# Modulation weights requested ahead of x, first quarter unsplit, norm copies on ACT, another order of the first blocks in a hybrid attention and retention layer

## The chip, the cores and the metric

One core of a Trainium2 chip. The metric is the device time of one execution in microseconds, lower is better; the median of several executions is given. The core has a matrix engine (TensorE, PE), three engines for the rest (VectorE or DVE, ScalarE or ACT, GpSimd or POOL), each of which takes its instructions strictly in order, and queues that move data between memory and the on-chip buffer (the SyncE queue, SP, carries nearly all of them here).

## The reference, cut to what matters

One layer over 2048 latent tokens and 256 context tokens of width 1024: a norm, a modulation computed from the condition vector, one input projection, two groups of heads, an output projection and a last norm. The change touches only the path up to the first projections:

```python
mod = jax.nn.silu(c) @ w_ada[i] + b_ada[i]
mod_c = jax.nn.silu(c_ctx) @ w_ada[i] + b_ada[i]
shift, scale, gate = mod[:, None, :D], mod[:, None, D:2 * D], mod[:, None, 2 * D:]
h_lat = _rmsnorm(x, norm_g[i]) * (1.0 + scale) + shift
h_ctx = _rmsnorm(ctx, norm_g[i]) * (1.0 + scale_c) + shift_c
...
na_q, na_k, na_v, na_g, r_q, r_k, r_v, r_g = _split_proj(h_lat @ w_in)
```

## The kernel before, in words

Matrix products are made of pairs: a number is kept as a rounded high part and the rest as a low part, and a product is high x high + low x high + high x low. So every operand needs a cast (high, on ACT) and a subtraction (low, on DVE or POOL) before PE can use it.

**Blocks and parts.** x comes transposed, in eight parts of 256 tokens (x 0 to x 7; part 8 is the context). Two parts make a block of 512 tokens (`blk[0]` to `blk[3]`, tiles `hhi` and `hlo` for high and low). The 1024 features are eight slices k of 128; half u of a part is k = 4u to 4u + 3.

**Modulation.** The weights w_ada come in four quarters u of four pieces j (`ada_load`, 512 KB each). Quarter u gives shift and scale of k = 2u and 2u + 1. A piece is multiplied by the condition on PE (`ada_mm`, `'m'`, L311) either as plain fp32 or, if its bit in `SPL` is set, as high and low part (`ada_split`, `'s'`, ACT L298, then DVE or POOL L300 by `ALO`). `ada_row` (`'ar'`, L319) copies the result out, `ada_fin` (`'af'`) transposes it on PE (L324) and DVE makes `mods` of it (L329 to L332).

**Norm.** `squares` (`'sq'`) squares a part on ACT (L198) and adds slices on POOL (half 0) and DVE (half 1), L200, L201 and a last addition on DVE, L203. `colsum` (`'cs'`, PE L209), `rstd` (DVE L214, POOL L215), `spread_copy` (DVE L220, both in `'rs'`) and `spread` (`'sp'`, PE L227) make the norm's factor for every token; `spread_mul` (`'mu'`, DVE L241) multiplies it in.

**Scale, shift and split.** For block 0 slice by slice: `prep_first(k)` (`'p'`: ACT L262 writes the high part, DVE L263 scales in place, DVE or POOL L265 the low part by `PFL`). For later blocks half by half: `prep_ab` (`'ab'`, DVE L272 and ACT L274) and `prep_hl` (`'hl'`, ACT L279, then DVE or POOL L283 by `LOV`).

**Key steps.** The first projections are the keys: `window(b)` runs, for block b, four units (two weight groups w0 and w1 of 256 columns, two halves each) of eight slices. A step is one slice of one unit: three matmuls at L363. For block 0 the order of units is the table `STEPS`; for the others unit after unit. Steps are numbered 32 b + n. Low parts of w0 and w1 (tile `wlo`, L347) are made by `w_split` (`'ws'`), on POOL or DVE by `WSL`.

**What sets the order.** `PLAN` is a list written out by hand: (step, action, arguments). After each step's matmuls the actions due at it are issued; those at -1 come ahead of step 0. The engines then run their own instructions in that order and wait only for data, a free buffer or a landed transfer. `LOADS` is the order of the first requests on the SP queue, which land one after the other. Stores and spills of finished blocks (`hS`) share that queue.

Of the kernel before, what the change touches and what calls it, by code (L numbers as in the profile page):

```python
# [9 lines left out]
F32 = mybir.dt.float32  # L10
# [3 lines left out]
ALU = mybir.AluOpType  # L14
# [4 lines left out]
P = 128  # L19
D = 1024  # L20
KC = D // P
# [15 lines left out]
TSQ = {0: 2, 1: 2, 2: 2, 3: 2, 4: 2, 5: 3, 6: 2, 7: 2, 8: 2}  # L37
LOV = {0: 2, 1: 2, 2: 0, 3: 3, 4: 2, 5: 2, 6: 1, 7: 3, 8: 0}
PLAN = [
# [19 lines left out]
]  # L59
SPL = [9, 0, 1, 0]  # L60
ALO = [0, 5, 9, 4]
PFL = [3, 0, 0, 1, 0, 3, 1, 3]
STEPS = [0, 1, 2, 0, 1, 3, 2, 3, 2, 0, 3, 1, 1, 3, 0, 3, 2, 3, 0, 0, 2, 1, 1, 1, 1, 2, 3, 2, 2, 0, 3, 0]
WSL = [3, 2]
LEAD = 32
LOADS = [
# [3 lines left out]
]  # L70
BT = [[(KWIN[i][1] * CWIN[j][1], 0, 0) for j in (0, 1, 3)] for i in (0, 1, 3)]
BN = 0
# [10 lines left out]
def hybrid_kernel(ctx: ExitStack, tc: tile.TileContext, a: dict, out: bass.AP):  # L83
# [22 lines left out]
    ng = cst.tile([P, KC], F32, name="ng")  # L106
    bada = cst.tile([P, 2 * KC], F32, name="bada")
    sil4 = cst.tile([P, KC, 4], F32R, name="sil4")
    mods = cst.tile([P, 4, 3, 2, 2], F32, name="mods")
    one = cst.tile([P, 1], F32, name="one")  # L110
    mhalf = cst.tile([P, 4], F32, name="mhalf")
# [82 lines left out]
    def squares(i):  # L194
        sqs[i] = []
        for u in range(2):
            sq = xsq[i][u] if i < 2 else env["st"].tile([P, KH, 256], F32, name="st")
            nc.scalar.activation(sq, raw[i][u], AF.Square)  # L198
            eng = (nc.gpsimd, nc.vector)[u]
            eng.tensor_tensor(sq[:, 0:2, :], sq[:, 0:2, :], sq[:, 2:4, :], ALU.add)  # L200
            eng.tensor_tensor(sq[:, 0, :], sq[:, 0, :], sq[:, 1, :], ALU.add)  # L201
            sqs[i].append(sq)
        nc.vector.tensor_tensor(sqs[i][0][:, 0, :], sqs[i][0][:, 0, :], sqs[i][1][:, 0, :], ALU.add)  # L203
# [13 lines left out]

    def spread_copy(i):
        rbs[i, 1] = env["st"].tile([P, 2, P], F32, name="t0", bufs=2)
        nc.vector.tensor_copy(rbs[i, 1], rbs[i].unsqueeze(2).to_broadcast([P, 2, P]))  # L220

    def spread(*ii):
        pm = ptile()
# [31 lines left out]
    def prep_first(k):  # L255
        if k == KC - 1:
            spill.extend((i, u, now[0] + 8) for i in range(2) for u in range(2))
        for i in range(2):
            hi, lo = sub_dst(i)
            A, B = ab(i, k)  # L260
            x = raw[i][k // KH][:, k % KH, :]
            nc.scalar.activation(hi[:, k, :], x, AF.Identity, bias=B, scale=A)  # L262
            nc.vector.tensor_scalar(x, x, A, B, ALU.mult, ALU.add)  # L263
            eng = nc.gpsimd if PFL[k] >> i & 1 else nc.vector
            eng.tensor_tensor(lo[:, k, :], x, f(hi[:, k, :]), ALU.subtract)  # L265

    def prep_ab(i, u):
# [25 lines left out]
    def ada_split(u, j):  # L293
        whl[u, j] = []
        for k in range(2):
            w = wad[4 * u + j][:, k, :]
            t = op.tile([P, 2, 512], F32R, name="o")
            nc.scalar.copy(t[:, 0, :], w)  # L298
            eng = nc.gpsimd if ALO[u] >> j & 1 else nc.vector
            eng.tensor_tensor(t[:, 1, :], w, f(t)[:, 0, :], ALU.subtract)  # L300
            whl[u, j].append(t)

    def ada_mm(u, j):
        if u not in aps:
            aps[u] = ptile(psm)
        for k in range(2):
            ops = [(silc, wad[4 * u + j][:, k, :])]
            if SPL[u] >> j & 1:
                ops = [(sil4, whl[u, j][k][:, e, :]) for e in range(2)]
            for i, (s, w) in enumerate(ops):  # L310
                nc.tensor.matmul(aps[u][0:s.shape[2], :], s[:, 2 * j + k, :], w, start=(j == 0 and i == 0 and k == 0),  # L311
                                 stop=(j == 3 and i + 1 == len(ops) and k == 1))
# [3 lines left out]
    def ada_row(u):  # L316
        rows[u] = op.tile([P, 2, 512], F32, name="o")[:, 0, :]
        n = 4 if SPL[u] else 2
        (nc.scalar.copy, nc.vector.tensor_copy)[u % 2](rows[u][0:n, :], aps[u][0:n, :])  # L319

    def ada_fin(u):
        pm, n = ptile(psm), 4 if SPL[u] else 2
# [127 lines left out]
        put_tok(rvS, c0, tp, r)  # L450

    nc.sync.dma_start(silc, a["c2"])
    nc.scalar.activation(silc, silc, AF.Silu)
    nc.scalar.copy(sil4[:, :, 0:2], silc)
    nc.vector.tensor_tensor(sil4[:, :, 2:4], silc, f(sil4[:, :, 0:2]), ALU.subtract)
    nc.vector.memset(one, 1.0)
# [8 lines left out]
    for name, *args in LOADS:  # L465
# [1 line left out]
    acts = dict(sq=squares, cs=lambda *i: colsum(*i), rs=lambda i: (rstd(i), spread_copy(i)), sp=lambda *i: spread(*i),  # L467
                mu=lambda i, u: spread_mul(i, (u,)), ab=prep_ab, hl=prep_hl, blk=alloc_blk, x=load_x, w=lambda: wr.append(w_raw(2560)),
                w2=lambda: load_w(), s=ada_split, m=ada_mm, ar=ada_row, af=ada_fin, p=prep_first,
                ws=lambda g: w01.append(w_split(wr[g], lo=WSL[g])))  # L470
    w01 = []

    def run_acts(n):
        while plan and plan[0][0] <= n:
# [1149 lines left out]
```

## Time and profile before

| | us |
|---|---|
| median of 3 runs | 1368.17 |
| lowest, highest | 1365.89, 1369.72 |
| the profiled execution | 1366.09 |
| its span, first to last instruction | 1364.1 |
| PE busy, to 27.4 us from the start | 17.09 |
| PE busy, 27.4 to 60.4 | 30.62 of 33.0 |
| PE busy, 60.4 to 85 | 22.26 of 24.6 |
| DVE busy, 60.4 to 85 | 21.79 of 24.6 |

A timeline row reads: start in us from the start of the span, time in us, engine, line, operation, output <- inputs, sizes and types, count of merged instructions; in brackets the idle time of the engine just before it and what ended it. Overlapping matmuls each show more than the distance between their starts. A windows row gives a stretch, its length, the busy time and number of instructions, the TensorE clock granted (1 is full), the share of the DMA engines and GB/s. An engine's "busy" time includes time in which it is held up inside an instruction. PE shows an unsplit modulation matmul as two records.

### The profile page before, as it was taken

The numbers are of one execution on the slowest core, as the hardware profiler recorded it, in microseconds if no ns is written. First come the engines' busy times: TensorE is split into PE (matmuls) and PEld (weight loads), VectorE is DVE, ScalarE is ACT, GpSimd is POOL, SyncE is SP. The second block draws the span as 40 slices with busy tenths as digits, with TensorE's granted clock in tenths as the row PEclk, the third lists the DMA queues.
The fourth block names the chain that finished last, engine by engine and source line by source line (L and its number), as shares of the span: only waits on it lengthen the run. The fifth ranks groups of instructions, "written<-read, shape, count | busy, mean of one in ns | idle before, by whom it ended". The sixth has DMA issues, their size and how long they took to land.

```text
span 1364.1 us, 23087 instructions
## 1 busy us (share of the span) xinstructions
PE 1313.1 (96%) x8236; PEld 1148.9 (84%) x8236; DVE 827.9 (61%) x1442; ACT 606.5 (44%) x1259; POOL 583.8 (43%) x571
## 2 busy tenths in 40 slices
PE   6999999999999999999999999999999899999997
PEld 2477899887997788998999889889998789888886
DVE  5686356675766754377767777776644633445345
ACT  5354343243533344555655466556642234333332
POOL 5452102554034664355535465555422254544432
PEclk9999999999999999999999999999999999999999
DMA  9386788464867657967587778676538988455533
GB/s 364 132 277 232 260 296 222 165 208 151 326 179 228 217 197 230 273 198 194 157 225 208 210 202 245 171 215 188 140 110 277 267 264 286 159 170 170 162 121 128
DMA packets 197685, 287.25 MB, mean 211 GB/s; under 512 B 17345, under 2 KB 126017, under 8 KB 196290
## 3 DMA queue, kind: packets, MB, share of 16 engines
q1 hardware_dynamic: 165154, 228.35, 56.4%
q10 hardware_dynamic: 32416, 57.42, 11.7%
q8 instruction: 66, 1.08, 0.3%
q14 instruction: 49, 0.40, 0.1%
HBM read 194.48 MB, written 91.23 MB: 209 GB/s over the span
## 4 chain that ended last, share of the span: by engine, by line
PE 70%; DMA 9%; DVE 8%; ACT 4%; POOL 3%; issue 3%; SPq 2%; ACTq 0%; POOLq 0%; DVEq 0%
PE mm L374 17%; PE mm L671 13%; PE mm L1465 11%; PE mm L363 7%; PE sS L1025 4%; PE tr L1052 3%; PE po L1073 3%; PE mm L1188 2%; PE tr L1054 2%; PE po L1075 2%; DMA vB<-o 1%; PE mm L1377 1%; PE mm L1376 1%; PE mm L1375 1%; PE mm L311 1%
## 5 line engine op out<-in xcount | busy, mean ns | idle before, releaser
L374 PE MATMUL mm<-whi,hlo 128*128 128x256 f32 x832 | 228.5, 282 | 0.2 <-DMA hlo<-cS 0.2
L374 PE MATMUL mm<-whi,hhi 128*128 128x256 f32 x768 | 224.2, 292 | 0.0
L374 PE MATMUL mm<-wlo,hhi 128*128 128x256 f32 x768 | 216.9, 282 | 0.0
L1056 ACT CAST pt<-tr 128x640 fp32r<-128x640 f32 (+1 forms) x128 | 95.6, 747 | 160.9 <-PE tr L1054 158.4
L1062 DVE TENSOR_TENSOR pt<-tr,pt 128x640 fp32r<-128x640 f32 (+1 forms) x128 | 113.9, 890 | 78.5 <-ACT pt L1056 77.2
L374 PEld LDWEIGHTS mm<-whi,hlo 128*128 128x128 f32 x832 | 156.3, 190 | 0.6 <-DMA hlo<-cS 0.5
L1045 POOL TENSOR_SCALAR sp<-sp,stt 128x640 f32<-128x640 f32 (+2 forms) x128 | 103.2, 808 | 106.5 <-DVE stt L1044 74.5
L374 PEld LDWEIGHTS mm<-whi,hhi 128*128 128x128 f32 x768 | 146.2, 190 | 0.0
L374 PEld LDWEIGHTS mm<-wlo,hhi 128*128 128x128 f32 x768 | 145.9, 190 | 0.1
L1034 DVE CUSTOM_DVE_ANT_0 sp<-sS,nb 128x640 f32<-128x640 f32 (+2 forms) x128 | 105.6, 825 | 33.6 <-PE sS L1025 27.2
L1039 ACT ACTIVATE sp<-sp,stt 128x640 f32<-128x640 f32 (+2 forms) x128 | 107.4, 839 | 19.9 <-DVE stt L1034 18.7
L625 POOL TENSOR_TENSOR whi<-st,whi 128x512 fp32r<-128x512 f32 x48 | 63.9, 1353 | 107.3 <-ACT whi L624 107.3
L363 PE MATMUL mm<-hhi,whi 128*128 128x512 f32 x256 | 107.8, 421 | 0.0
L363 PE MATMUL mm<-hlo,whi 128*128 128x512 f32 x256 | 101.6, 397 | 6.0 <-DVE hlo L265 2.1
L1025 PE MATMUL sS<-k,q 128*128 128x256 f32 (+3 forms) x512 | 99.0, 315 | 5.3 <-DVE stt L1034 5.0
L363 PE MATMUL mm<-hhi,wlo 128*128 128x512 f32 x256 | 101.9, 398 | 0.3 <-DVE wlo L347 0.3
L671 PE MATMUL mm<-hhi,whi 128*128 128x512 f32 x336 | 98.4, 395 | 3.7 <-POOL whi L625 3.2
L1474 DVE TENSOR_TENSOR xt<-mm,xt 128x512 f32<-128x512 f32 x64 | 43.8, 686 | 87.4 <-PE mm L1465 87.3
L1465 PE MATMUL mm<-wor,y 128*128 128x512 f32 x384 | 95.6, 398 | 1.1 <-DVE xt L1474 1.1
L1025 PEld LDWEIGHTS sS<-k,q 128*128 128x128 f32 x512 | 82.7, 188 | 12.2 <-DVE stt L1034 8.4
L1465 PE MATMUL mm<-won,y 128*128 128x512 f32 x336 | 89.9, 406 | 0.0
L625 POOL TENSOR_TENSOR wlo<-st,wlo 128x512 fp32r<-128x512 f32 x36 | 53.6, 1488 | 77.4 <-ACT wlo L624 77.4
(258 smaller groups left out, 3057.5 us busy)
## 6 DMA issues: line engine op xcount, KB each, us to landing
st<-in_w_in_dram SPq DMA_DIRECT2D x64, 512.0 KB
q<-qS SPq DMA_DIRECT2D x64, 256.0 KB
hlo<-hS SPq DMA_DIRECT2D x20, 512.0 KB
k<-kS SPq DMA_DIRECT2D x16, 576.0 KB
kS<-o SPq DMA_DIRECT2D x16, 512.0 KB
vB<-o SPq DMA_DIRECT2D x64, 128.0 KB
qS<-o ACTq DMA_DIRECT2D x16, 512.0 KB
woS<-g ACTq DMA_DIRECT2D x32, 256.0 KB
```

The source lines that it names most:

```text
L363: nc.tensor.matmul(pm[:, :n], ww[:, k, cs], h[:, k, :], start=(k == 0 and i == 0), stop=(k == KC - 1 and i == 2))
L374: nc.tensor.matmul(pm[:, t * WG:(t + 1) * WG], h[:, k, o:o + P], ww[:, k, :], start=(k == 0 and i == 0), stop=(k == KC - 1 and i == 2))
L625: nc.gpsimd.tensor_tensor(t[:, 1], r, f(t)[:, 0], ALU.subtract)
L671: nc.tensor.matmul(pm, ww[:, k, :], hh[:, k, :], start=(k == 0 and i == 0), stop=(k == KH - 1 and i == 2))
L1025: nc.tensor.matmul(o, hd["q"][i][:, hl, j * P:(j + 1) * P], k, start=(hl == 0), stop=(hl == 1))
L1034: nc.vector.tensor_tensor_reduce(T["sp"][:, :n], T["s"], nbz[big][:, o:o + n], -1.0, 3e38, ALU.add, ALU.min, T["st"][:, 0:1])
L1039: nc.scalar.activation(sp[:, :n], sp[:, :n], AF.Exp, bias=st[:, 0:1], scale=-1.0, accum_out=st[:, 1:2])
L1045: nc.gpsimd.tensor_scalar(sp[:, :n], sp[:, :n], st[:, 2:3], 0.0, ALU.mult, ALU.add)
L1056: nc.scalar.copy(pt[:, :ng_ + 2, 0, :], tr[:, :ng_ + 2, :])
L1062: nc.vector.tensor_tensor(pt[:, :n, 1, :], tr[:, :n, :], f(pt)[:, :n, 0, :], ALU.subtract)
L1465: nc.tensor.matmul(pm, yy[:, k, :], ww[:, k, sl], start=(k == 0 and i == 0), stop=(k == 3 and i == 2))
L1474: nc.vector.tensor_tensor(xts[t][:, sl], pm, xts[t][:, sl], ALU.add)
```

## The change

What it does:

- `LOADS`: the first three pieces of quarter 0 are requested ahead of x; w0 and w1 keep about their place.
- `SPL`: quarter 0 is no longer split; of all pieces only (3, 0) and (3, 2) are. Unsplit pieces of a split quarter use a condition padded with zeros (`silz`), so that all rows of the result are written.
- `spread_copy` of parts 0 and 1 goes from DVE to ACT; `squares` of parts 0 and 1 adds on DVE alone; low parts of part 1 in `prep_first` are always POOL's and those of part 0 DVE's; in a split the low part is always DVE's; rows of quarters 1 to 3 are copied out by ACT.
- the low parts of w0 and w1 are all POOL's, and each group is made in two halves that the plan places apart (`ws_half`).
- `STEPS`: the four units of block 0 advance together.
- `PLAN`: another order up to step 41. The sums of squares of part 4 go from step 13 to step 25, their column sums from 23 to 33; block 1 is scaled and cast at steps 14 to 24 instead of 24 to 29. From step 42 on the plan is the same.

```diff
-    (4, 's', 2, 0), (4, 'x', 4), (4, 'p', 2), (5, 'sq', 2), (7, 'm', 2, 0), (8, 'm', 2, 1), (9, 'p', 3),
...
+    (-1, 'm', 0, 0), (-1, 'm', 0, 1), (-1, 'm', 0, 2), (-1, 'sq', 1), (-1, 'm', 0, 3), (-1, 'cs', 1), (-1, 'rs', 1),
+    (-1, 'ar', 0), (-1, 'sq', 0), (-1, 'm', 1, 0), (-1, 'af', 0), (-1, 'sp', 1), (-1, 'cs', 0), (-1, 'rs', 0),
...
-SPL = [9, 0, 1, 0]
-ALO = [0, 5, 9, 4]
-PFL = [3, 0, 0, 1, 0, 3, 1, 3]
-STEPS = [0, 1, 2, 0, 1, 3, 2, 3, 2, 0, 3, 1, 1, 3, 0, 3, 2, 3, 0, 0, 2, 1, 1, 1, 1, 2, 3, 2, 2, 0, 3, 0]
-WSL = [3, 2]
+SPL = [0, 0, 0, 5]
+STEPS = [0, 1, 0, 1, 2, 3, 2, 3, 0, 1, 2, 3, 0, 1, 2, 3, 0, 1, 2, 3, 0, 1, 2, 3, 0, 0, 1, 1, 2, 2, 3, 3]
...
-    ('x', 1), ('a', 0, 1), ('a', 0, 0), ('x', 0), ('a', 0, 3), ('a', 0, 2), ('c',), ('a', 1, 0), ('w', 0),
+    ('a', 0, 0), ('a', 0, 1), ('a', 0, 2), ('x', 1), ('c',), ('a', 0, 3), ('x', 0), ('a', 1, 0), ('a', 1, 1), ('w', 0), ('a', 1, 2),
...
-            eng = (nc.gpsimd, nc.vector)[u]
+            eng = nc.vector if u or i < 2 else nc.gpsimd
...
-        nc.vector.tensor_copy(rbs[i, 1], rbs[i].unsqueeze(2).to_broadcast([P, 2, P]))
+        copy = nc.scalar.copy if i < 2 else nc.vector.tensor_copy
+        copy(rbs[i, 1], rbs[i].unsqueeze(2).to_broadcast([P, 2, P]))
...
-        for i in range(2):
+        for i in (1, 0):
...
-            eng = nc.gpsimd if PFL[k] >> i & 1 else nc.vector
+            eng = nc.gpsimd if i else nc.vector
...
-            eng = nc.gpsimd if ALO[u] >> j & 1 else nc.vector
-            eng.tensor_tensor(t[:, 1, :], w, f(t)[:, 0, :], ALU.subtract)
+            nc.vector.tensor_tensor(t[:, 1, :], w, f(t)[:, 0, :], ALU.subtract)
...
-            ops = [(silc, wad[4 * u + j][:, k, :])]
+            ops = [(silz if SPL[u] else silc, wad[4 * u + j][:, k, :])]
...
-        (nc.scalar.copy, nc.vector.tensor_copy)[u % 2](rows[u][0:n, :], aps[u][0:n, :])
+        (nc.scalar.copy if u else nc.vector.tensor_copy)(rows[u][0:n, :], aps[u][0:n, :])
...
-                ws=lambda g: w01.append(w_split(wr[g], lo=WSL[g])))
-    w01 = []
+                ws=lambda g, u: ws_half(g, u))
+    w01, wps = [], {}
+
+    def ws_half(g, u):
+        if u == 0:
+            w, wps[g] = w_parts(wr[g])
+            w01.append(w)
+        wps[g][u]()
```

ACT at the start of the program, before the first key step; `st` holds raw projection weights, `t_...` the norm's copy, `mm` a result of PE. Before:

```order
L198 ACTIVATE hhi<-hhi 128x1024 x2
L298 CAST o<-hhi 128x512 x2
L198 ACTIVATE hhi<-hhi 128x1024 x2
L298 CAST o<-hhi 128x512 x2
L319 COPY o<-mm 4x512
L345 CAST whi<-st 128x1024 x2
L262 ACTIVATE hhi<-hhi,mods 128x256 x4
```

And now, where the lines of the program have moved by up to two (squares are L196, casts of the weights L343, scaling L261, row copies L317):

```order
L196 ACTIVATE hhi<-hhi 128x1024 x2
L219 COPY t_208<-rs 128x256
L196 ACTIVATE hhi<-hhi 128x1024 x2
L219 COPY t_238<-rs 128x256
L343 CAST whi<-st 128x1024
L261 ACTIVATE hhi<-hhi,mods 128x256 x4
L343 CAST whi<-st 128x1024
L317 COPY o<-mm 2x512
L343 CAST whi<-st 128x1024
```

The squares of the second part now stand behind the norm's copy of the first, and the first cast of the weights behind the copy of the second; the other casts are spread out.

POOL from the roots of parts 0 and 1 on; `wlo` are low parts of the weights, `hlo` of x. Before:

```order
L215 TENSOR_TENSOR rs<-rs,mhalf 128x2 x2
L347 TENSOR_TENSOR wlo<-st,whi 128x1024 x2
L265 TENSOR_TENSOR hlo<-hhi 128x256 x2
L347 TENSOR_TENSOR wlo<-st,whi 128x1024
L300 TENSOR_TENSOR o<-hlo,o 128x512 x2
L200 TENSOR_TENSOR st<-st 128x512
L201 TENSOR_TENSOR st<-st 128x256
```

And now:

```order
L213 TENSOR_TENSOR rs<-rs,mhalf 128x2 x2
L345 TENSOR_TENSOR wlo<-st,whi 128x1024
L264 TENSOR_TENSOR hlo<-hhi 128x256 x2
L345 TENSOR_TENSOR wlo<-st,whi 128x1024 x2
L264 TENSOR_TENSOR hlo<-hhi 128x256 x2
L345 TENSOR_TENSOR wlo<-st,whi 128x1024
L198 TENSOR_TENSOR st<-st 128x512
L199 TENSOR_TENSOR st<-st 128x256
```

POOL has four halves of `wlo` instead of three, and w0's second half and w1's first stand between the low parts of x for k = 0, 1 and those for k = 2, 3.

DVE around the last quarter of the modulation. Before, the last rows of slices and sums, roots, and then the modulation (L329, L332):

```order
L263 TENSOR_SCALAR hhi<-hhi,mods 128x256
L265 TENSOR_TENSOR hlo<-hhi 128x256
L200 TENSOR_TENSOR st<-st 128x512
L201 TENSOR_TENSOR st<-st 128x256
L203 TENSOR_TENSOR st<-st 128x256
L214 TENSOR_SCALAR rs<-mm 128x2
L220 COPY t_447<-rs 128x256
L319 COPY o<-mm 2x512
L214 TENSOR_SCALAR rs<-mm 128x2
L220 COPY t_457<-rs 128x256
L329 TENSOR_TENSOR mods<-mm,bada 128x8
L332 SCALAR_TENSOR_TENSOR mods<-mods,ng 128x4
```

And now, from the last row of that modulation (L330) to the next sums:

```order
L330 SCALAR_TENSOR_TENSOR mods<-mods,ng 128x4
L282 TENSOR_TENSOR hlo<-hlo,hhi 128x4x256
L262 TENSOR_SCALAR hhi<-hhi,mods 128x256 x2
L264 TENSOR_TENSOR hlo<-hhi 128x256
L262 TENSOR_SCALAR hhi<-hhi,mods 128x256 x2
L264 TENSOR_TENSOR hlo<-hhi 128x256
L240 TENSOR_TENSOR hlo<-hlo,mm 128x1024 x2
L271 TENSOR_SCALAR hlo<-hlo,mods 128x256 x4
L282 TENSOR_TENSOR hlo<-hlo,hhi 128x4x256
L198 TENSOR_TENSOR st<-st 128x512
L199 TENSOR_TENSOR st<-st 128x256
L201 TENSOR_TENSOR st<-st 128x256
```

The three sums of squares of part 4 (L200, L201, L203, now L198, L199, L201) stood ahead of the last quarter's modulation; now they stand behind it, behind the last slices of block 0 and behind the second half of block 1.

More of the change, by code (lines that the diff above doesn't have):

```diff
@@ L39 @@
 PLAN = [
[19 rows of a table removed]
-]
-SPL = [9, 0, 1, 0]
-ALO = [0, 5, 9, 4]
-PFL = [3, 0, 0, 1, 0, 3, 1, 3]
-STEPS = [0, 1, 2, 0, 1, 3, 2, 3, 2, 0, 3, 1, 1, 3, 0, 3, 2, 3, 0, 0, 2, 1, 1, 1, 1, 2, 3, 2, 2, 0, 3, 0]
-WSL = [3, 2]
[20 rows of a table added]
+]
+SPL = [0, 0, 0, 5]
+STEPS = [0, 1, 0, 1, 2, 3, 2, 3, 0, 1, 2, 3, 0, 1, 2, 3, 0, 1, 2, 3, 0, 1, 2, 3, 0, 0, 1, 1, 2, 2, 3, 3]
 LEAD = 32
 LOADS = [
[3 rows of a table removed]
+    ('a', 0, 0), ('a', 0, 1), ('a', 0, 2), ('x', 1), ('c',), ('a', 0, 3), ('x', 0), ('a', 1, 0), ('a', 1, 1), ('w', 0), ('a', 1, 2),
+    ('a', 1, 3), ('w', 1), ('a', 2, 0), ('a', 2, 1), ('x', 2), ('a', 2, 2), ('a', 2, 3), ('x', 3), ('a', 3, 0), ('a', 3, 1), ('a', 3, 2), ('a', 3, 3),
 ]
@@ L108, in hybrid_kernel @@
     sil4 = cst.tile([P, KC, 4], F32R, name="sil4")
+    silz = cst.tile([P, KC, 4], F32, name="silz")
     mods = cst.tile([P, 4, 3, 2, 2], F32, name="mods")
@@ L452, in hybrid_kernel @@
     nc.sync.dma_start(silc, a["c2"])
+    nc.vector.memset(silz, 0.0)
     nc.scalar.activation(silc, silc, AF.Silu)
+    nc.vector.tensor_copy(silz[:, :, 0:2], silc)
     nc.scalar.copy(sil4[:, :, 0:2], silc)
```

38 rows, old and new, of tables (LOADS, PLAN) are left out of this document.

## The prediction

> **What bounds the kernel now.** The page first: TensorE (PE) is busy in 96% of the span, all but the first slice nearly full, and every other engine is under two thirds.
>
> ```profile
> span 1364.1 us, 23087 instructions
> PE 1313.1 (96%) x8236; PEld 1148.9 (84%) x8236; DVE 827.9 (61%) x1442; ACT 606.5 (44%) x1259; POOL 583.8 (43%) x571
> PE   6999999999999999999999999999999899999997
> ```
>
> So a change counts only by what it does to the instants at which PE has nothing to do, or runs at half clock. The change rewrites the work up to step 41 of the plan (one step is three key matmuls); from step 42 on the plan is the same. I therefore read the timeline of PE to the sums of squares of block 5, which follow step 42, and then the timelines of DVE, POOL and ACT beside it.
>
> ```profile
> 27.44 0.49 PE L363 MATMUL mm<-hhi,whi 128*128 128x512 f32 x1
> 37.88 0.50 PE L363 MATMUL mm<-hlo,whi 128*128 128x512 f32 x1 [1.70 <-DVE hlo L265]
> 60.35 0.41 PE L324 MATMUL mm<-ident,o 2*128 2x2 f32 x4
> 76.01 0.57 PE L363 MATMUL mm<-hlo,whi 128*128 128x512 f32 x1 [1.96 <-DVE hlo L283]
> 84.98 0.50 PE L209 MATMUL mm<-one,st 128*128 128x1 f32 x4
> 102.53 0.50 PE L363 MATMUL mm<-hlo,whi 128*128 128x512 f32 x1 [1.45 <-POOL hlo L283]
> 39.00:42.00 3.00, 3.00 (x5) 0.50 1.04 414
> 76.00:80.00 4.00, 3.99 (x11) 0.57 1.00 260
> ```
>
> Step 0 starts at 27.44, the last quarter of the modulation is transposed (L324) at 60.35, step 42 is over at 84.98. In between PE waits twice for a low part, 1.70 and 1.96 us, and behind each of these waits the granted clock is 0.50 for a while (the fourth number of the two windows rows; 39 to 42 is all of it, and of 76 to 80 about 3.4 us). Half clock for 3.4 us costs 1.7 us. The two waits are thus worth 1.70 + 1.96 + 2 x 1.7 = 7.1 us. The wait of 1.45 at 102.53 was followed by no half clock.
>
> **What sets the low parts: DVE and POOL take turns.**
>
> ```profile
> 33.76 0.40 DVE L263 TENSOR_SCALAR hhi<-hhi,mods 128x256 f32<-128x256 f32 x1
> 35.53 1.37 DVE L263 TENSOR_SCALAR hhi<-hhi,mods 128x256 f32<-128x256 f32 x1
> 35.28 1.46 POOL L200 TENSOR_TENSOR st<-st 128x512 f32<-128x512 f32 x1
> 36.82 0.72 POOL L201 TENSOR_TENSOR st<-st 128x256 f32<-128x256 f32 x1
> 76.39 2.80 DVE L283 TENSOR_TENSOR hlo<-hlo,hhi 128x1024 fp32r<-128x1024 f32 x1
> 74.65 1.21 DVE L283 TENSOR_TENSOR hlo<-hlo,hhi 128x1024 fp32r<-128x1024 f32 x1
> 75.30 2.81 POOL L283 TENSOR_TENSOR hlo<-hlo,hhi 128x1024 fp32r<-128x1024 f32 x1 [1.68 <-ACT hhi L279]
> 20.67 4.67 POOL L347 TENSOR_TENSOR wlo<-st,whi 128x1024 fp32r<-128x1024 f32 x2 [0.41 <-ACT whi L345]
> 66.51 2.34 DVE L241 TENSOR_TENSOR hlo<-hlo,mm 128x1024 f32<-128x1024 f32 x2
> ```
>
> The same DVE scale takes 0.40, and 1.37 where it ends with POOL's sum; the same DVE subtraction takes 1.21, and 2.80 where POOL's runs until 78.11. So I lay operations of these two with SBUF inputs end to end, in turns. From the short rows I take: DVE scale 0.36, DVE subtraction 0.42 (256 wide) and 1.2 (1024), POOL 0.73 (256), 1.15 (512), 2.33 (1024, half of 4.67), and the multiplications by the norm, 1.17 each.
>
> **Up to step 0: no gain.** Requests land one after the other; this row and two more fix the pace.
>
> ```profile
> 5.56 1.06 ACT L198 ACTIVATE hhi<-hhi 128x1024 f32<-128x1024 f32 x1 [2.62 <-DMA hhi<-in_xT_dram]
> 13.57 1.14 ACT L298 CAST o<-hhi 128x512 fp32r<-128x512 f32 x2 [0.30 <-DMA hhi<-in_w_ada_dram]
> 12.27 4.84 PE L311 MATMUL mm<-hhi,silc 128*2 128x512 f32 x8
> 42.90 3.60 PE L311 MATMUL mm<-hlo,silc 128*2 128x512 f32 x8
> 34.87 1.09 PE L311 MATMUL mm<-o,sil 128*4 128x512 f32 x4
> 18.36 0.71 POOL L215 TENSOR_TENSOR rs<-rs,mhalf 128x2 f32<-128x2 f32 x1 [3.78 <-DVE rs L214]
> 19.11 0.29 DVE L220 COPY t<-rs 128x256 f32<-128x256 f32 x1 [0.83 <-POOL rs L215]
> 61.56 0.60 ACT L262 ACTIVATE hhi<-hhi,mods 128x256 fp32r<-128x256 f32 x1 [7.85 <-DVE mods L332]
> ```
>
> The first and the seventh half megabyte are used at 5.56 and 13.57: 1.3 us each. In the new order the fourth quarter piece is sixth (12.3), x of block 1 fourth and fifth (9.5, 10.8), x of block 0 seventh and eighth (13.6, 14.9), the first projection weights eleventh (18.8), the last piece of the second quarter fourteenth (22.7). PE gets work at 5.6 instead of 10.2. An unsplit piece takes 1.8 us (3.60 for two), 3.4 at half clock; a split one 1.09. Ahead of step 0 the eight pieces take 1.4 us more than before (two splits fewer), behind it 0.7 us less (one more).
>
> PE holds the column sums of block 1 behind the sixth request, to 14.5; DVE 0.15, POOL 0.71 and the ACT copy follow to 16.8. ACT's copy isn't in this trace: at most the 0.60 of an ACT row of that width, at least DVE's 0.29; I take 0.55, and the difference is 0.3 us, twice on the path. Only behind it stand the squares of block 0 (ACT, in order), 2 x 1.06, so they end at 18.9 though x was there at 14.9. DVE sums to 20.5, column sums 21.0, root and copy 22.7, spread 23.3, multiply 24.5. On PE the last three unsplit pieces of quarter 1 follow the column sums of block 0: 21.0 + 0.6 + 3 x 1.8 = 27.0. **Step 0 starts at 27.0, as before** (bounds 25.5 to 28.7: PE's clock in the first ten microseconds).
>
> **Steps 0 to 11: a wait at step 4.** POOL now has all four halves of the weights' low parts, in the order: w0 first half, the two low parts of block 1, w0 second half, w1 first half. ACT's cast of the first half waits behind the norm's copy, so POOL starts at 23.8 (20.67 before). With DVE's turns between: 26.1; DVE's two scales 26.8, POOL 27.6, DVE 28.0; the next round 29.9; two halves 34.6 (33.2 if DVE gets fewer turns). PE needs w1's half at its third matmul of step 4, at 31.5: **wait 3.1 us**, and half clock. Then steps 5 to 7, four unsplit pieces (7.2), steps 8 to 11: 48.9 with the half clock. Meanwhile DVE and POOL do k = 2 and 3, the last weight half and the sums of blocks 2 and 3: 34.6 + 4.9 + 2.4 + 6.8 = 48.7. Both arrive together at the column sums of blocks 2 and 3.
>
> **Steps 12 to 17.** DVE is in order: modulation 2 (0.5), a split (1.28, as its row shows), k = 4 (1.9 with POOL), two roots with copies (1.4 each with POOL), k = 5 (1.9), two multiplications (2.4), a second split (1.28), to 60.9.
>
> ```profile
> 15.31 1.28 DVE L300 TENSOR_TENSOR o<-hhi,o 128x512 fp32r<-128x512 f32 x2
> 82.03 0.39 PE L363 MATMUL mm<-hhi,wlo 128*128 128x512 f32 x1
> 82.25 0.39 PE L363 MATMUL mm<-hhi,whi 128*128 128x512 f32 x1
> ```
>
> PE alone (0.69 a step, three of the gaps between the last two rows) would be at that second split at 58.0. It ends at 61.2; one unsplit piece and two steps follow: the last quarter's transposes at 64.4 to 64.75, against 60.35 to 60.76: **4.0 us late**.
>
> **Steps 18 to 42: the wait before step 34.** Call the end of these transposes T. DVE then has, in order: modulation (0.65), the low part of block 3 (1.2), k = 6 and 7 with POOL (3.75), two multiplications (2.4), four scales (1.5): T + 9.5. ACT scales and casts to T + 10.2 and 11.2, POOL subtracts block 2's second half to T + 12.6, DVE block 3's to T + 13.8, and only then come the sums of squares of block 4, in turns: 1.15 + 0.69 + 0.73 + 0.42 + 0.43 = T + 17.2.
>
> ```profile
> 37.75 0.68 DVE L200 TENSOR_TENSOR st<-st 128x512 f32<-128x512 f32 x1
> 38.46 0.42 DVE L201 TENSOR_TENSOR st<-st 128x256 f32<-128x256 f32 x1
> 38.97 0.43 DVE L203 TENSOR_TENSOR st<-st 128x256 f32<-128x256 f32 x1
> 74.17 1.99 ACT L279 CAST hhi<-hlo 128x1024 fp32r<-128x1024 f32 x2 [0.64 <-DVE hlo L272]
> 71.22 0.68 DVE L384 TENSOR_TENSOR o<-mm,o 128x512 fp32r<-128x512 f32 x1
> ```
>
> PE, in order too, meets their column sums behind step 33, at T + 11.7 (sixteen steps and 0.6 for k = 7): **wait 5.6 us**, then half clock. In before these sums stood ahead of modulation 3 on DVE and nothing waited for them. Behind them DVE has four evictions (0.68 each, the third behind a key store, since two output tiles rotate), so the root of block 4 is spread at T + 24.3, the next wait; step 42 ends at T + 27.5 = 92.2. Before: 84.98. **Sum: 92.2 - 85.0 = 7.2 us later**, of which 4.0 before T and 3.2 behind. From the spread at step 50 DVE is free again by these sums, and the waits from 102.53 on recur. The profiled execution took 1366.09, the median is 1368.17; the sum goes onto the median, 1375.
>
> **Rivals.** (A) Faster: block 1 (tokens 512 to 1023) is cast and subtracted at steps 16 to 24 instead of 28 to 29, so the wait of 1.96 and the clock loss behind it go; the plan's earlier sums of blocks 2 and 3 take away the wait of 1.70. This decides if the squares of block 4 are summed by PE's step 33 and DVE doesn't hold the second split. Then 7.1 + 0.7 go, and the wait at step 4, half as long, stays with its clock: 1.5 + 1.7. 1368.2 - 4.6 = 1363.6. For it: PE alone is 3 to 5 us ahead by step 24. Against: the turns of 1.37 and 2.80. [...]
>
> (B) No change: DVE's turns overlap PE more than I lay them, T is 61.5, the wait for block 4 is 4 us: 0.7 + 1.6, 1370.5.
>
> (C) The start moves: with PE at full clock early and the copy at 0.29, step 0 comes at 25.5; but POOL's start moves only with the copy, by 0.6, so the wait at step 4 takes the rest. It is inside the forecast's range, as is step 0 at 28.7.
>
> **How the numbers follow.** Forecast (slower) 0.62, B 0.26, A 0.12. The forecast alone: each of its three stages is good to about 2 us, 1371 to 1380. The range, 1364 to 1381, takes in B and cuts most of A. A measurement of this kernel tells about 0.3% (4.1 us) from no change: faster 0.12, same 0.28, slower 0.60, the forecast giving a little of its chance to "same".
>
> **What would show it.** Right: the first key matmul near 27; a wait of about 3 us on POOL's wlo at the fifth step; the last L322 transposes at 64 to 65; a wait of some 5 us on DVE at the column sum behind step 33, granted clock 0.5 behind it. Wrong: no such wait, or the transposes before 61 (A); DVE scales that overlap POOL at 0.36 (B); a wait that is new from step 50 on, where I have none.

## The result, and the profile after

The kernel after took **1378.55 us** (median of 6, 1373.74 to 1382.04), the kernel before 1365.88 us in the runs beside it (median of 6, 1362.77 to 1369.72). The ratio is 1.0092, 95% interval 1.0070 to 1.0114: the change makes the kernel slower, by some 12.7 us. The page of after, the lines that answer to those of before:

```profile
span 1376.6 us, 23083 instructions
PE 1318.4 (96%) x8236; PEld 1154.0 (84%) x8236; DVE 830.2 (60%) x1443; ACT 606.5 (44%) x1260; POOL 579.3 (42%) x566
```

PE is busy 5.3 us longer (1318.4 against 1313.1) with the same number of instructions, for which the longer half clock below is enough; the rest of the 12.5 us of span is waiting. The timeline of PE in after (start, duration, operation, and in brackets the idle time ahead of it with what ended it):

```profile
28.74 0.50 PE L361 MATMUL mm<-hhi,whi 128*128 128x512 f32 x1
34.42 0.50 PE L361 MATMUL mm<-hhi,wlo 128*128 128x512 f32 x1 [1.63 <-POOL wlo L345]
60.88 0.41 PE L322 MATMUL mm<-ident,o 4*128 4x4 f32 x4
77.18 1.01 PE L207 MATMUL mm<-one,st 128*128 128x1 f32 x4 [4.71 <-DVE st L201]
87.97 1.19 PE L226 MATMUL mm<-ident,t 128*128 128x128 f32 x4 [4.22 <-DVE t L219]
93.44 0.50 PE L207 MATMUL mm<-one,st 128*128 128x1 f32 x4
110.99 0.50 PE L361 MATMUL mm<-hlo,whi 128*128 128x512 f32 x1 [1.48 <-POOL hlo L282]
116.51 1.18 PE L226 MATMUL mm<-ident,t 128*128 128x128 f32 x4 [1.59 <-DVE t L219]
183.42 0.58 PE L372 MATMUL mm<-whi,chi 128*128 128x256 f32 x1 [4.00 <-ACT whi L343]
```

Each row is laid beside the same instruction of before. Step 0 is at 28.74 (27.44 before, 1.3 us late), the last quarter's transposes at 60.88 (60.35, 0.5 late), the column sums of part 5, which end step 42, at 93.44 (84.98, 8.5 late), the low part of block 2 at 110.99 (102.53, 8.5 late). So nearly all that is lost by then is lost between 61 and 93, in the waits of 4.71 and 4.22 us. The last wait, for `whi` at 183.42, is new too (PE waits 0.50 there in before). Two more rows of PE's timeline of each kernel, the first of the context keys (chi) and one from the stage behind; before:

```profile
152.59 0.28 PE L363 MATMUL mm<-chi,whi 128*128 128x256 f32 x1
301.51 2.73 PE L671 MATMUL mm<-hlo,wlo 128*128 128x512 f32 x11
```

and after:

```profile
162.38 0.28 PE L361 MATMUL mm<-chi,whi 128*128 128x256 f32 x1
315.61 2.73 PE L677 MATMUL mm<-hlo,wlo 128*128 128x512 f32 x11
```

9.8 us late at the first, 14.1 at the second: the context stage loses another 4.3. (The 1.3 us between 8.5 and 9.8 are lost behind the wait of 1.59 at 116.51.) Of the 14.1, 1.6 come back by the end (12.5 in the spans), in small pieces that were not followed up.

The stretches at half clock in after, in the view of windows (stretch, its length, busy time of PE, PEld, DVE, ACT and POOL, then the granted clock, the DMA share and GB/s):

```profile
75.80:82.60 6.80, 5.42 (x15) 4.48 (x16) 3.11 (x5) 0.59 (x1) 0.52 (x1) 0.51 0.55 201
86.10:92.90 6.80, 4.92 (x14) 4.14 (x15) 5.06 (x7) 2.01 (x4) 2.84 (x3) 0.52 1.04 378
116.80:120.20 3.40, 3.40 (x13) 2.85 (x12) 1.62 (x4) 0.00 (x0) 0.23 (x1) 0.54 0.61 219
181.60:188.40 6.80, 4.52 (x20) 4.23 (x21) 4.85 (x5) 4.37 (x5) 0.00 (x0) 0.51 0.45 139
```

Each of the three waits of 4.0 us and more is followed by, and partly lies in, 6.8 us at half clock, twice what before had behind its waits of 1.70 and 1.96.

### The profile page after: what moved, and what is told of

The parts are those of the page before. It is cut to its first block, busy times and chain, and to the rows that moved or that the text cites. A ratio compares the mean times of both kernels' runs of the same rounds, so it can differ in the third digit from the quotient of the medians.

```text
span 1376.6 us, 23083 instructions
## 1 busy us (share of the span) xinstructions
PE 1318.4 (96%) x8236; PEld 1154.0 (84%) x8236; DVE 830.2 (60%) x1443; ACT 606.5 (44%) x1260; POOL 579.3 (42%) x566
## 4 chain that ended last, share of the span: by engine, by line
PE 46%; DVE 6%; DMA 6%; POOL 5%; issue 4%; ACT 3%; SPq 2%; ACTq 1%; POOLq 0%; DVEq 0%
PE mm L1471 11%; PE mm L372 10%; PE sS L1031 5%; PE mm L361 3%; PE tr L1058 3%; PE po L1079 3%; PE mm L1194 2%; DMA woS<-g 2%; PE tr L1060 2%; PE po L1081 2%; DMA v<-rvS 1%; POOL g L765 1%; PE mm L1383 1%; PE mm L1382 1%; PE mm L1381 1%
```

## The experiments

"Theory" in the expectations is at first the prediction's: the loss is the place of part 4's squares on DVE and what follows from it. Every ratio is to the kernel before in the same runs.

### Early sums: the squares of part 4 ahead of the last quarter

```diff
-    (13, 's', 3, 2), (14, 'ab', 2, 0), ... (24, 'hl', 3, 1), (25, 'sq', 4), (33, 'cs', 4), (33, 'rs', 4),
+    (13, 's', 3, 2), (13, 'sq', 4), (14, 'ab', 2, 0), ... (23, 'cs', 4), (24, 'hl', 3, 1), (24, 'rs', 4),
```

> The changed kernel with one thing undone: the sums of squares of part 4 stand at step 13 again (behind the split of piece (3, 2)) and their column sums at 23 instead of 33. Theory (order): the 4.71 us wait at L207 behind step 33 and the half clock behind it go, and the key results' eviction no longer stands behind those squares on ACT, so that the 4.22 us wait for the spread shrinks below 1 us; the column sums of part 5 come near 86 (93.4 changed, 85.0 before); about 1371 beside 1378.5 and 1366, or 0.4% over before. Rival (start): the loss comes from POOL's low parts of the weights and the new request order ahead of step 8; then hardly anything comes back, 1376 to 1379.

1376.27 us, ratio 1.0084 (1.0050 to 1.0117). About 1371 was expected; the median is only 2.3 us under that of after, and the intervals of the two ratios overlap. The two waits for part 4 are gone, but one for part 5 has come. Its row, and two of ACT:

```profile
87.78 0.98 PE L207 MATMUL mm<-one,st 128*128 128x1 f32 x4 [8.02 <-DVE st L201]
79.48 0.59 ACT L381 CAST o<-mm 128x512 fp32r<-128x512 f32 x1 [6.74 <-DMA kS<-o]
83.29 2.00 ACT L196 ACTIVATE st<-hhi 128x1024 f32<-128x1024 f32 x2
```

The squares of part 5 (L196) start only at 83.29: on ACT they stand behind four evictions of key results, and the third of these waits 6.74 us until the first key store has left one of the two output tiles. The loss had a second layer: block 0's four units end within six steps, and two tiles can't take four results.

### Less work for POOL ahead of step 4

```diff
-            w, wps[g] = w_parts(wr[g])
+            w, wps[g] = w_parts(wr[g], lo=(3, 2)[g])
```

> The changed kernel with the low part of the first half of w1 on DVE again (lo=(3, 2)[g] in ws_half). Theory (order): the wait of 1.63 us at step 4 goes, DVE gets 1.2 us more, the waits at steps 33 and 38 stay; 1 to 2 us back at most, about 1377. Rival (start): several us back, 1372 or less.

1379.24 us, ratio 1.0093 (1.0065 to 1.0121). The wait at step 4 falls from 1.63 to 0.98, and nothing comes of it that these runs can tell: the wait for part 4 (4.72 us) ends at 77.07, where it was.

### The kernel before with part 4's squares late

```diff
-    (13, 'sq', 4), ... (23, 'cs', 4), (24, 'rs', 4), ... (28, 'sp', 4), ... (29, 'mu', 4, 0), (31, 'sq', 5), (34, 'mu', 4, 1),
+    ... (29, 'sq', 4), (33, 'cs', 4), (33, 'rs', 4), (36, 'sq', 5), (38, 'sp', 4), (38, 'mu', 4, 0), (40, 'mu', 4, 1),
```

> The kernel before with one thing of the change: the sums of squares of part 4 behind block 1's second half (step 29) and their column sums at 33, spread at 38, multiplications at 38 and 40. Theory (order): a wait of 4 us or more at the column sums behind step 33 with half clock behind it, while the wait of 1.96 us at step 32 stays; 6 to 9 us slower than before, about 1373. Rival (start): within 2 us of before, 1366 to 1368.

1373.04 us, ratio 1.0059 (1.0037 to 1.0081), as the theory had it: 7.5 us over before, from the changed places of the actions on parts 4 and 5 alone (the scaling of part 4, `ab`, goes from step 39 to 41 too). The wait is after's:

```profile
79.54 1.01 PE L209 MATMUL mm<-one,st 128*128 128x1 f32 x4 [4.91 <-DVE st L203]
```

In the context stage this kernel has no wait for `whi`.

### After with the requests of before

```diff
-    ('a', 0, 0), ('a', 0, 1), ('a', 0, 2), ('x', 1), ('c',), ('a', 0, 3), ('x', 0), ...
+    ('x', 1), ('a', 0, 1), ('a', 0, 0), ('x', 0), ('a', 0, 3), ('a', 0, 2), ('c',), ...
```

> The changed kernel with the request order of before (x of block 1 first, pieces of the four quarters mixed). Theory (order): step 0 moves by 2 us or less either way (28.7 changed, 27.4 before) and the waits at steps 33 and 38 stay, 1376 to 1380. Rival (start): 4 us or more back, 1374 or less.

1381.54 us, ratio 1.0113 (1.0087 to 1.0140), above the theory's range. Step 0 moves by 4.8 us, to 33.58, where at most 2 was expected; everything up to the wait for part 4 is late by that (the wait ends at 81.72 instead of 77.18), and the wait is as long (4.69). So in these two executions the new order of requests is worth 4.5 us up to there. Some 1.2 of them may be the clock: ahead of step 0 the rows of PE for the same work are longer than in after (column sums 0.99 us against 0.67, the next unsplit piece 3.57 against 3.44, the transposes 1.22 against 0.71, the last two pieces 3.84 against 3.60). In the medians it is 3.0, and the intervals of the two ratios overlap. The rest of the change costs more than it brings.

### Squares of part 5 ahead of the evictions

Early sums as above, and `(36, 'sq', 5)` becomes `(24, 'sq', 5)`.

> The kernel after with the sums of squares of part 4 at step 13 (as in the run before it with early sums) and, new, the squares of part 5 at step 24, ahead of the four evictions of block 0, instead of at step 36 behind them. Theory (the squares stood on ACT behind evictions that wait for key stores to land, since two output tiles rotate): the wait of 8.02 us at the column sums of part 5 and its half clock (10.2 us at half, 5.1 lost) go, no wait above 2 us is left between 60 and 100 us, and some 8 to 13 us of the 1376.3 come back: 1364 to 1369. The evictions come 2 us later, which nobody on PE waits for. Rival (the limit is the sum of work on DVE and POOL in this stretch, not the order on ACT): the wait only moves on to the spread of part 4 or the low parts of block 2, 1373 to 1377.

1374.40 us, ratio 1.0068 (1.0042 to 1.0094): a miss, in the rival's range. The wait at the column sums of part 5 is gone, but PE waits at the next thing that DVE has behind the evictions:

```profile
98.00 1.22 PE L226 MATMUL mm<-ident,t 128*128 128x128 f32 x4 [9.86 <-DVE t L219]
93.69 0.59 ACT L381 CAST o<-mm 128x512 fp32r<-128x512 f32 x1 [6.70 <-DMA kS<-o]
```

The stores went out later still, and the root of part 5 (DVE, in order) stood behind block 1's first eviction. So the squares' place was not the limit; the next run asks whether the stores were.

### Four output tiles in block 0

```diff
-        o = op.tile([P, 2, 512], F32R, name="o")
+        late = b == 0 and c0 == 768
+        o = env["st"].tile([P, 2, 512], F32R, name="st") if late else op.tile([P, 2, 512], F32R, name="o")
```

> The kernel after with the outputs of the last two key units of block 0 in tiles of the pool of the squares, so that four output tiles stand ready instead of two and no eviction of block 0 waits for a store. Theory (the third and fourth eviction wait for the stores, and DVE, in order, holds the root of part 4 behind them): the wait at the column sums of part 4 stays (4.7 us, half clock behind it), the wait of 4.22 us at the spread of part 4 and its half clock go: 7 us back, 1370 to 1373. Rival (DVE's own work holds the root): the spread wait stays within 1 us, 1377 to 1380.

1371.99 us, ratio 1.0040 (1.0023 to 1.0058), as the theory had it. The first wait stays, the second is gone (the row has no bracket):

```profile
76.72 1.01 PE L207 MATMUL mm<-one,st 128*128 128x1 f32 x4 [4.70 <-DVE st L201]
83.05 0.61 PE L226 MATMUL mm<-ident,t 128*128 128x128 f32 x4
```

So the wait of 4.22 us was the stores, not DVE's own work.

### Early sums and four output tiles

Both edits together.

> The kernel after with the sums of squares of part 4 at step 13 and the four output tiles, squares of part 5 still at step 36. Theory: neither the wait for part 4 nor the stores are left, squares of part 5 start near 76 instead of 83.3, and the wait of 8.02 us at the column sums of part 5 shrinks to 0 to 2.5 us without the long half clock: 1364 to 1370. Rival (work, not order): the wait stays above 5 us, 1374 or more.

1370.44 us, ratio 1.0038 (1.0026 to 1.0051), just above the forecast. Both layers are gone: the column sums of part 5 wait 0.56, and come at 80.60 (84.98 in before). What is new stands at block 2; here are three rows of PE and the one of ACT behind them:

```profile
80.60 0.58 PE L207 MATMUL mm<-one,st 128*128 128x1 f32 x4 [0.56 <-DVE st L201]
99.29 0.50 PE L361 MATMUL mm<-hhi,whi 128*128 128x512 f32 x1 [2.76 <-ACT hhi L278]
103.22 0.80 PE L361 MATMUL mm<-hlo,whi 128*128 128x512 f32 x1 [3.42 <-POOL hlo L282]
96.30 2.94 ACT L278 CAST hhi<-hhi 128x1024 fp32r<-128x1024 f32 x3 [6.55 <-DMA hS<-hhi]
```

Block 2's high part takes the buffer of parts 0 and 1, and these must first be spilled (`hS<-hhi`). In the changed plan the first half of block 1 (both parts) is split ahead of block 0's last slice. So two of block 1's four spills come into the list first, block 0's four stand behind them in the SP queue, and block 1's other two come last. The first three spills in SP's rows of after (block 1 lies in `hlo`, block 0 in `hhi`):

```profile
57.82 0.39 SPq L252 DMA_DIRECT2D hS<-hlo  x1
78.44 0.59 SPq L252 DMA_DIRECT2D hS<-hlo  x1
82.42 0.45 SPq L252 DMA_DIRECT2D hS<-hhi  x1
```

The waits at block 2 use up the lead of 4.4 us, but hardly more than that: the first matmul of the context keys comes 0.3 us behind before's. What is lost in the end is lost behind it, in the context stage; these rows stand beside 152.59 and 301.51 in before:

```profile
152.86 0.28 PE L361 MATMUL mm<-chi,whi 128*128 128x256 f32 x1
305.99 2.73 PE L678 MATMUL mm<-hlo,wlo 128*128 128x512 f32 x11
```

### The wait in the context stage: addresses?

From the third context eviction on the wait is for the first store of context keys (256 columns wide). Its row in before, and in after:

```profile
166.39 0.37 ACT L383 CAST o<-mm 128x256 fp32r<-128x256 f32 x1 [4.47 <-DMA kS<-o]
```

```profile
177.96 0.37 ACT L381 CAST o<-mm 128x256 fp32r<-128x256 f32 x1 [6.35 <-DMA kS<-o]
```

Behind it ACT casts the weights that PE waits for. The requests of that stage are the same, in the same order. The windows over the 4 us in which block 1 is read back (`hhi<-hS`) end in GB/s; before, then after:

```profile
157.60:161.60 4.00, 4.00 (x36) 4.00 (x35) 1.02 (x2) 2.06 (x3) 0.00 (x0) 1.00 0.99 349
```

```profile
167.40:171.40 4.00, 4.00 (x37) 4.00 (x36) 1.13 (x2) 2.16 (x3) 0.00 (x0) 1.00 0.92 235
```

Over the same transfer DMA moves 349 and 235 GB/s at shares of 0.99 and 0.92, and the store behind it lands later (the eviction waits 4.47 and 6.35 us for it). Two runs ask whether places decide it. The kernel before with an unused tile (128 bytes per partition, so that on-chip addresses are after's):

```diff
+    silz = cst.tile([P, KC, 2 * 2], F32, name="silz")
     mods = cst.tile([P, 4, 3, 2, 2], F32, name="mods")
```

> The kernel before with one unused tile of 128 bytes per partition where the kernel after has silz, so that all tiles behind it lie at the addresses that they have in the kernel after. It tests the wait of 4.0 us for whi in the context stage, where both kernels issue the same requests in the same order. Theory of the address: eviction three of the context keys waits over 6 us for the first context key store, and PE waits some 4 us for whi: 1369 to 1371. Rival (the address does nothing): the wait on the store stays at 4 to 5 us, PE's at 0.8, 1364 to 1367.

and early sums with four tiles, and an unused array ahead of the spilled blocks in memory:

```diff
+    pad = dram.tile([P, 5120], F32, name="pad")
     hS = [dram.tile([P, KC, 512], F32, name=f"hS{b}") for b in range(4)]
```

> The kernel with early sums and four output tiles, and an unused array of 2.6 MB declared ahead of the spilled blocks in memory, so that these lie elsewhere. In the context stage the reload of block 1 runs at 205 to 266 KB per us in the kernels with the changed plan, and at 303 to 377 in those with the plan before, with the same requests in the same order. Theory of the place in memory: the reload goes at over 300 KB per us, eviction three waits 3.5 to 4.5 us instead of 5.6, PE waits under 1 us for whi, 1363 to 1367. Rival (the place does nothing): PE waits about 3 us for whi, 1369 to 1372.

The first took 1363.17 us, ratio 0.9975 (0.9959 to 0.9992), the second 1368.73, ratio 1.0034 (1.0017 to 1.0051). The rates (first, second):

```profile
157.30:161.30 4.00, 4.00 (x37) 4.00 (x36) 0.97 (x2) 2.00 (x3) 0.00 (x0) 1.00 1.02 351
```

```profile
159.00:163.00 4.00, 4.00 (x37) 4.00 (x36) 0.88 (x2) 1.92 (x3) 0.00 (x0) 1.00 0.93 240
```

Neither rate is far from that of its kernel without the shift (349, and 231 with early sums and four tiles): both theories of the place fall. (That an unused tile gives 0.9975 also shows what a difference of a quarter per cent is worth here.)

### Block 0's spills first

Early sums and four output tiles, and:

```diff
-            spill.extend((i, u, now[0] + 8) for i in range(2) for u in range(2))
+            spill[0:0] = [(i, u, now[0] + 5) for i in range(2) for u in range(2)]
```

> The kernel with early sums and four output tiles, and the four spills of block 0 put ahead of block 1's in the list and due five steps behind the last slice instead of eight. It is about the two waits that this kernel got at the first key matmuls of block 2 (2.76 us for the high part, 3.42 us for the low part, 6.8 us of half clock), whose ACT cast waited 6.55 us until the tile of the first two parts was spilled. Theory (the spills of block 0 stand behind block 1's and the key stores in the SP queue): the cast waits less than 1 us, the two waits together fall under 2 us, and 4 to 8 us come back: 1363 to 1367 if the wait of some 3 us for whi in the context stage stays. Rival (the casts are late by DVE's multiplications, not by the spills): the waits stay within 1 us of what they were, 1369 to 1372. For the context stage there is no forecast: that block 0's spills stand first, as in the kernel before, is one of the differences left that could lie behind it.

1363.12 us, ratio 0.9991 (0.9974 to 1.0008): level with before. ACT's cast, PE's wait at block 2, and the window of the reload:

```profile
92.61 2.95 ACT L278 CAST hhi<-hhi 128x1024 fp32r<-128x1024 f32 x3 [2.57 <-DMA hS<-hhi]
99.58 0.50 PE L361 MATMUL mm<-hlo,whi 128*128 128x512 f32 x1 [2.50 <-POOL hlo L282]
159.00:163.00 4.00, 4.00 (x37) 4.00 (x36) 0.93 (x2) 1.96 (x3) 0.00 (x0) 1.00 1.01 366
```

The cast waits 2.57 instead of 6.55 (under 1 was expected), the two waits at block 2 come to 2.50 and 0.76 (under 2 together was expected). What had no forecast: the reload runs at 366 GB/s, and the wait for `whi` is gone. The same two matmuls as above show where the gain lies:

```profile
153.85 0.28 PE L361 MATMUL mm<-chi,whi 128*128 128x256 f32 x1
301.79 2.73 PE L678 MATMUL mm<-hlo,wlo 128*128 128x512 f32 x11
```

By the first context key the edit has brought nothing: it comes 1.0 us later than without it, since half clock is still there at block 2 (a matmul takes 0.63 us to 111.34, 0.40 from 112.16 on) and a wait of 1.59 is new at 106.08. By the second matmul it has brought 4.2. So the time fell into the expected range by luck: it was not the waits that the edit was made for that gave the time back.

### The same in the kernel after, alone

The last edit, put into the kernel after.

> The kernel after with nothing changed but the order of the spills: block 0's four go ahead of block 1's four in the list (and are due five steps behind the last slice instead of eight). Theory (this order alone decides how fast block 1 is reloaded in the context stage; how it does so is open): the reload goes at over 300 KB per us, the third context eviction waits 3.5 to 4.5 us for its store instead of 6.35, PE waits under 1 us for whi instead of 4.0 and keeps its full clock there; the waits of 4.7 and 4.2 us near 77 and 88 stay: 1378.5 less 3 to 4 of wait and 3.4 of half clock, 1370 to 1373. Rival (in the run with early sums, four output tiles and this order it was the time of the spills, or the tiles, or chance): PE waits 3 to 4 us for whi, 1376 to 1380.

1370.65 us, ratio 1.0059 (1.0030 to 1.0089), as the theory had it. The interval overlaps that of after (1.0070 to 1.0114), so the rows must carry the reading. The waits for part 4 are still there (4.70 and 4.47 us; behind the second the half clock lasted 3.4 us in this execution, not 6.8, which is 1.7 of the 7.9 us). The first context key comes at 160.56 (162.38 in after), the matmul that after has at 315.61 at 308.56: 5.2 us come back in the context stage, which is before's again:

```profile
178.82 0.38 PE L372 MATMUL mm<-wlo,chi 128*128 128x256 f32 x1 [0.76 <-DVE wlo L345]
165.60:169.60 4.00, 4.00 (x36) 4.00 (x35) 1.04 (x2) 2.07 (x3) 0.00 (x0) 1.00 1.00 347
```

The place of the spills in the list therefore decides the rate of the reload some 75 us later (347 GB/s here, 235 in after). The edit also makes block 0's spills due three steps earlier; the kernel before keeps the eight steps and is fast, which speaks for the order. The order moves the first spill too (57.82 in after, 77.14 here), and the runs don't tell these two apart. How it does so, with the same bytes at the same places, stays open.

### A try at beating both

Early sums, four output tiles, block 0's spills first, and two low parts moved from POOL to DVE (`lo=(3, 2)[g]` as above, and `LOV[4]` from 2 to 3).

> The kernel with early sums, four output tiles and block 0's spills first, and two low parts moved from POOL to DVE: the first half of w1's low part is POOL's and the second DVE's, and part 4's second low half (LOV of part 4 from 2 to 3) DVE's. It is meant to beat both kernels. Theory (POOL had two subtractions of 2.4 us each in a row at 94.7 and PE waited 2.50 us for the second; the last half of w1 stood behind three others on POOL): the wait of 2.50 us at the first matmuls of block 2 falls under 1 us, the wait of 2.22 us at step 4 under 1 us, half clock behind them goes: 1358 to 1362. Rival (DVE, which scales part 5 at that time, is then late by as much): 1362 to 1365.

1365.97 us, ratio 1.0012 (0.9994 to 1.0029): no gain, just above the rival's range. The two waits fall to 1.00 and 1.32 (under 1 was expected):

```profile
31.62 0.50 PE L361 MATMUL mm<-hhi,wlo 128*128 128x512 f32 x1 [1.00 <-DVE wlo L345]
98.81 0.51 PE L361 MATMUL mm<-hlo,whi 128*128 128x512 f32 x1 [1.32 <-POOL hlo L282]
```

Others of the same size stand beside them, 1.52 us on DVE's sums at 46.62 and 1.40 on ACT's cast at 103.03, and there is still half clock at block 2 (0.63 us for the matmul at 109.75). No version was found that beats the kernel before by more than can be measured.

## Why the prediction was right, and where not

The direction, the wait for part 4 and the range held; that the time fell so near is partly luck. The sum of 7.2 us stands against 12.7 measured, and its errors pulled against each other: T (the end of the last quarter's transposes) was laid 3.5 us too late, the stretch from T to step 42 4.8 us too short, and the 4.3 us of the context stage were not in it. The sum was also put onto 1368.17, where the kernel before took 1365.88 beside the new one, so the time is 2.3 us nearer than the difference. Of the signs named for being right, only the wait on part 4 came as written. Of those named for being wrong, two came: the transposes before 61, and a new wait behind step 50.

**Step 0.** 27.0 was forecast, 28.74 came, at the upper bound. The window of 21.2 to 24.6 us ran at half clock, ahead of step 0, which costs 1.7:

```profile
21.20:24.60 3.40, 3.40 (x6) 0.37 (x5) 1.29 (x2) 1.85 (x3) 1.59 (x2) 0.53 1.04 414
```

This belongs to the execution, not to the change. Nine more kernels profiled here have the changed requests and the same PE instructions ahead of step 0; in eight of them step 0 is at 26.38 to 26.85, in one at 28.59. So the step was right but for the clock, which the bounds allowed for.

**The wait at step 4.** POOL's two halves were put at 34.6, and PE got the last at 34.42; but PE itself came 1.3 us later than the forecast's 31.5, by the late step 0. So the wait is 1.63 instead of 3.1, with no half clock behind it; where step 0 came in time and POOL's share was the same, it is 2.20 to 2.22. The run with POOL's share moved shows no gain from it by itself.

**The second split and T.** This is the term that failed: T was to be 4.0 us late and is 0.5 late. DVE was to be done with the sums of parts 2 and 3 (the prediction calls them blocks) at 48.7 and with the second split at 61.2; the terms that it lists for the second stretch add up to 60.8, and the other 0.4 have no source. DVE's rows:

```profile
46.32 0.43 DVE L201 TENSOR_TENSOR st<-st 128x256 f32<-128x256 f32 x1
55.82 1.28 DVE L298 TENSOR_TENSOR o<-clo,o 128x512 fp32r<-128x512 f32 x2
```

They end at 46.7 and 57.1. From the wait at step 4 (34.4) to the first is 12.3 us, laid as 14.1; from there to the second 10.4, laid as 12.5. The error is mainly the method: DVE and POOL were laid end to end in turns, and they overlap more than that. The scales of k = 2, for one, ran from 32.75 to 34.85, while POOL was still at w1's half, and k = 4 took 1.6 us where 1.9 was laid.

**The wait for part 4.** T, the end of the transposes, is 61.29 (60.88 + 0.41). PE's arrival was put at T + 11.7 and is at T + 11.2 (77.18 - 4.71 - 61.29); the sums' end was put at T + 17.2 and is at T + 15.8 (77.13); so the wait was put at 5.6 and is 4.71. (The two rows shown for PE's pace start 0.22 apart, which is 0.66 a step and not the 0.69 used.) The kernel before with late squares shows the same wait and a loss of 7.5 us, and early sums take the wait away. This step was right.

**From there to step 42.** The second failed term: the spread was put at T + 24.3 and step 42's end at T + 27.5; they came at T + 26.7 and T + 32.2. The rows of ACT, and of DVE, in after:

```profile
73.26 1.05 ACT L381 CAST o<-mm 128x512 fp32r<-128x512 f32 x2
81.05 0.59 ACT L381 CAST o<-mm 128x512 fp32r<-128x512 f32 x1 [6.74 <-DMA kS<-o]
84.28 0.59 ACT L381 CAST o<-mm 128x512 fp32r<-128x512 f32 x1 [2.65 <-DMA kS<-o]
```

```profile
77.04 1.28 DVE L382 TENSOR_TENSOR o<-mm,o 128x512 fp32r<-128x512 f32 x2
84.90 0.69 DVE L382 TENSOR_TENSOR o<-mm,o 128x512 fp32r<-128x512 f32 x1 [2.54 <-ACT o L381]
86.47 1.35 DVE L219 COPY t<-rs 128x256 f32<-128x256 f32 x1 [0.82 <-POOL rs L213]
```

The prediction had the third eviction behind a store; the fourth is too, and no store can leave ahead of DVE's half of the eviction, which the sums hold to 77.04 (the first leaves at 77.75). With four tiles this wait goes. The copy of the root took 1.35 us, not 0.29. And the second wait was given no half clock of its own; it got 6.8 us of it at 0.52, which costs up to 3.4.

**From step 50 on** the prediction had nothing new. That was wrong by 1.3 us behind the wait at 116.51 (1.51 us with no half clock in before, 1.59 with 3.4 us of it here) and by the 4.3 us of the context stage. The cause of the second is a part of the change that the prediction didn't look at: splitting block 1 earlier puts two of its spills ahead of block 0's in the SP queue. The run with that order alone undone gives the stage back.

**The rivals.** Of A (faster), the waits of 1.70 and 1.96 did go, but its condition, that part 4's squares are summed by step 33, did not hold. B (no change) came nearest up to the wait: it had T at 61.5 and the wait at 4 us, measured 61.29 and 4.71. That the time did not stay within 0.3% is due to what neither had: the stores and the second half clock behind the wait, and the context stage.

**The half clock.** A wait of 1.63 us drew none at 34.42 (the clock is 1.00 from 33 to 37), one of 1.59 drew 3.4 us at 0.54 at 116.51. The same wait of 2.22 us at step 4, behind the same PE instructions, was followed by half clock in the run with early sums, four tiles and block 0's spills first (0.63 us a matmul from 33.95 to 36.51), and by none in the run with that order of spills alone. So the price of one wait in one execution says little.

## What to carry to other kernels

When work is moved to a later place, list the queue's requests that move with it as well as the engine's: here splitting half of block 1 ahead of block 0's last slice reordered a list of spills, and that cost 4.3 us in a stage some 75 us away. Where a wait goes in an experiment and the time stays, look for the next one in the same chain (sums, then output tiles) and undo them together; of the kernels run here with the changed plan, only those with sums, tiles and spills undone are level with before. And before a gain is put down to the wait that an edit was made for, lay the same instruction of both timelines side by side: here the gain of the spills came some 60 us behind the waits that they were moved for.

## What the runs showed of the hardware that was not expected

Over 4 us of the same reload of 2 MB, with the same requests around it, DMA moved 349 GB/s in before, 351 with the unused tile, and 366 and 347 in two runs with block 0's spills first; where two spills of block 1 come first it was 235 in after, 231 with early sums and four tiles, and 240 with the unused array, each in one execution and with a DMA share of 0.92 to 1.02. The half clock behind a wait was not the same in every execution: 3.4 us behind waits of 1.70 and 1.96 in before, 6.8 behind each of the three of 4.0 us and more in after, and 3.4 behind one of 4.47 in the kernel after with block 0's spills first.
